# One scan stage's order rewritten: the inverse loaded and transposed just ahead of its products, and a later stage's first products taken two pieces at a time

## The chip, the cores and the metric

The kernel runs on one core of one Trainium2 chip. The metric is the time on the device in microseconds (us), as the median of several runs; lower is better.

## The reference, cut to what matters

One step of a diffusion backbone with one layer. From normalised and modulated tokens (128 context tokens, 2048 latent ones, 1024 channels) one input projection makes all operands. Half of the channels go through an RWKV-7 recurrence, in both directions, with 8 heads of 64 channels:

```python
def step(S, inp):
    r_t, w_t, k_t, v_t, kk_t, a_t = inp
    s_kk = jnp.einsum('bdhij,bdhj->bdhi', S, kk_t)
    S = (S * w_t[..., None, :] - s_kk[..., :, None] * (kk_t * a_t)[..., None, :]
         + v_t[..., :, None] * k_t[..., None, :])
    return S, jnp.einsum('bdhij,bdhj->bdhi', S, r_t)
s_final, ys = lax.scan(step, s0.astype(f32), xs)
```

The other half is a gated short convolution. Both are gated, joined, projected out, added to the input and normalised. Everything is in float32.

## The kernel before, in words

**Three phases.** `phase1` makes the projections and writes the operands of the recurrence to memory. `phase2` is the recurrence, called the scan here. `phase3` is the output projection; some of its products are made within the last stages of the scan.

**How the scan is cut.** The tokens are cut into chunks of 64, and the recurrence over a chunk becomes matrix products: within a chunk a triangular system is solved, and only the 64 x 128 state of a pair of heads is carried from chunk to chunk. There are 17 stages (`NST`, line 618); a stage is eight chunks of one pair of heads in each direction, so two groups `g` per stage, forward and backward. Of a stage `s` these parts exist, all generators that hand back control at each `yield`:

- `partL` (line 789) loads the operands `rr`. `partM` (807) makes masked products of them: F, GA and Q. One pass over a group is four pieces, given by `MORD`: both halves of F ("Ff"); both halves of GA and the packed blocks dg, which ScalarE's queue stores to memory ("GgD"); nothing; the transposes Q. Each piece starts from block-diagonal copies `bd` made by ScalarE. With two groups that is eight pieces. `partI` (845) loads the blocks back as `ab` (line 850, SyncE's queue), and GpSimd solves for the first half of the inverse, `zt`, in 15 rounds (lines 864 to 870), and stores it (line 871).
- `partW` (873) loads that part of the inverse as `zc` and transposes it on VectorE into `zr` (line 879); then, in two halves, it loads strips of operands (`load_stk`, lines 779 and 782) and copies parts of GA and Q into them, and loads the values `sv`.
- `partU` (899) uses `zr` in the small products psU (line 905), their copy and `zc` in the products psW (912), and writes the whole inverse `zb`.
- `partB` (924), in two halves of three pieces: psX from `zb` and F (931), copies into the strips by ScalarE, and the products psE (942), masked by VectorE into E (943).
- `partS` (947) is the recurrence itself, eight scan steps numbered from 0: psS from E and the state (982), and VectorE's scaling of the state for the next step (995). After steps 3 and 7 the outputs `y` are copied or added (`outputs`, line 1002); `finish` completes a block of outputs.

**What sets the order.** `main` (line 1085) writes the stages' parts into one another by hand. In stage `s` it takes the scan steps of `s`. Before step 0 and after each step, `emit(k)` takes what the string at place `k` of `ORDER` names: L a half of `partW` of stage s+1, b and B a piece of `partB` (of stage s, second half, and of s+1, first half), U a piece of `partU` of s+1. Ahead of that, after every scan step, one piece of `partM` of stage s+3 (`LA` is 3) is taken, and after it, where there is one, a part of `finish`. At the end of the stage come `partL` of s+4 and `partI` of s+3. Stage 15, the last that has a next one, goes by `ORDER_END`.

The order in the code is not quite the order in the engines' queues. The context is opened with `schedule_with_timeline_sim=True` (line 1334): a scheduler plays the program against its own estimate of durations and puts onto each engine's queue what is ready by that estimate, the earlier in the code first. Once it is in a queue, the order is fixed: an instruction that waits holds up all that stand behind it on its engine. SyncE's queue issues nearly all loads and stores.

**Rings that bind pieces to one another.** `zc` and `zr` have one buffer each; the PSUM pool of psF, psG and psQ has two banks, and so has the pool of psU, psW, psX, psE and of the transposes in `finish`. `bd` and `rr` have two tiles. F, GA and Q have three slots, so that a later stage's F waits until psX of the stage three before has read it.

Of the kernel before, what the change touches and what calls it, by code (L numbers as in the profile page):

```python
# [620 lines left out]
LA = 3  # L621


ORDER_END = ("LbbbL", "U", "U", "", "BBB", "", "", "", "")
ORDER = ("LbbbL", "", "U", "", "U", "", "BBB", "", "")


def phase2(K):
    nc, tc, A, S = K.nc, K.tc, K.A, K.S
    V, G, P, T = nc.vector, nc.gpsimd, nc.scalar, nc.tensor  # L630
    D = nc.sync.dma_start
    MF, MG, ME = (0, 1), (0, 1), (2, 3)
    B = Ctx()
    O = Ctx()
# [73 lines left out]
    def copy(k, dst, src, negate=False):  # L708
        if negate:
            if k in ON_DVE:  # L710
                V.tensor_scalar(dst, src, -1.0, None, ALU.mult)
            else:
                P.activation(dst, src, AF.Copy, scale=-1.0)
        else:
            (V.tensor_copy if k in ON_DVE else P.copy)(dst, src)  # L715
# [16 lines left out]
    def tl(shape, tag, b, pool=None, dt=F32):  # L732
        return (pool or O.l0).tile(shape, dt, tag=tag, name=f"{tag}_{K.u()}", bufs=b)
# [21 lines left out]
    def load_v(dst, units):  # L755
        if units[0][0] == units[-1][0]:
            p, c0 = units[0]
            D(dst.rearrange("t u h v -> t u (h v)"), S["vt"][c0 * 64:(c0 + 8) * 64, p * 128:(p + 1) * 128].rearrange("(u t) c -> t u c", t=64))
        else:
            for u in range(2):  # L760
                D(dst.rearrange("t (g u) h v -> t u g (h v)", u=2)[:, u], S["vt"][u * 64:u * 64 + 64, :].rearrange("t (g c) -> t g c", g=4))
# [7 lines left out]
    def load_stk(t_, g, k, us):  # L769

        units = g.units[us]
        p, c0 = units[0]
        src = S[f"ops{g.d}"][k]
        n = 4 if p == units[-1][0] else 2
        for i in range(4 // n):
            dst = t_[0:64, 1, :, us.start + n * i:us.start + n * (i + 1)]
            x = src[(p + i) * 128:(p + i + 1) * 128, c0 * 64:(c0 + n) * 64]
            if t_ is g.rt:
                D(dst.rearrange("c h u t -> c h (u t)"), x.rearrange("(h c) t -> c h t", h=2))
            else:  # L780
                for hd in range(2):
                    D(dst[:, hd], x[hd * 64:hd * 64 + 64].rearrange("c (u t) -> c u t", t=64))

    def half(g, n):

        h = n if g.d == 0 else 1 - n
        return slice(h * 4, h * 4 + 4)

    def partL(s):
        st = Ctx()  # L790
        st.g = []
        for gi, (d, units, blk) in enumerate(stages[s]):
            g = Ctx()
            st.g.append(g)
            g.d, g.units, g.blk = d, units, blk
            g.rr = B.rr()
            if blk is None:
                for i, k in ((0, 0), (1, 1), (3, 2), (4, 3)):
                    load(g.rr[:, i], d, k, units, FULL)
            else:  # L800
                p, c0 = units[0]
                src = S[f"ops{d}"][:, p * 128:(p + 1) * 128, c0 * 64:(c0 + 8) * 64]
                for i, k in ((0, 0), (3, 2)):
                    D(g.rr[:, i:i + 2].rearrange("p k u t -> p k (u t)"), src[k:k + 2].rearrange("k p t -> p k t"))
        return st
# [66 lines left out]

    def partW(s, st):

        st.zc = tl([128, 16, 32], "zc", 1, O.l1)
        for h in range(2):
            D(st.zc[h:128:2], S["zt"][s][h].rearrange("u s b q i -> (s b q) u i"))
        st.zr = tl([128, 16, 32], "zr", 1, O.l1)
        V.transpose(st.zr[:].rearrange("p u i -> p (u i)"), st.zc[:].rearrange("p u i -> p (u i)"))
        for g in st.g:  # L880
            g.lt, g.rt = B.lt(), B.rt()
            g.fs, g.gs = (g.lt, g.rt) if g.d == 0 else (g.rt, g.lt)
            g.E = []
        for n in range(2):
            for g in st.g:
                us = half(g, n)
                load_stk(g.fs, g, 2, us)
                load_stk(g.gs, g, 1, us)
                for i in range(2):
                    r = slice(64 - i * 64, 128 - i * 64)  # L890
                    copy("g", g.gs[64:128, 1, i, us], g.GA[r, us, 0:64])
                    k = us.start // 2
                    copy("h", g.gs[64:128, 0, :, us.start + i:us.stop:2], g.Q[i * 64:i * 64 + 64, k:k + 2].rearrange("p k (h c) -> p h k c", h=2))
                if n == 0:
                    g.sv = tl([128, 8, 2, 64], "sv", 4)
                    load_v(g.sv[64:128], g.units)
            yield

    def partU(s, st):

        pu = O.p2.tile([128, 16, 32], F32, tag="s", name=f"psU{s}")
        rows = [(slice(sl * 64, sl * 64 + 32), slice(sl * 64 + 32, sl * 64 + 64)) for sl in range(2)]
        for u in range(16):
            for r0, r1 in rows:
                T.matmul(pu[r1, u, :], st.g[u // 8].GA[r0, u % 8, 96:128], st.zr[r0, u, :], start=True, stop=True)
        for r0, r1 in rows:
            copy("u", B.bu[r1], pu[r1])
        yield
        pw = O.p2.tile([128, 16, 32], F32, tag="s", name=f"psW{s}")
        for u in range(16):  # L910
            for r0, r1 in rows:
                T.matmul(pw[r0, u, :], B.bu[r1, u, :], st.zc[r1, u, :], start=True, stop=True)
        zf = B.zb[:].rearrange("p d u c -> p (d u) c")
        for r0, r1 in rows:
            for r in (r0, r1):
                copy("z", zf[r, :, r], st.zc[r])
            copy("n", zf[r0, :, r1], pw[r0], True)
        yield
# [156 lines left out]
    def first(s):  # L1075
        sts[s] = partL(s)
        yield from partM(s, sts[s])
        partI(s, sts[s])
# [6 lines left out]
    def main():  # L1085
        setup_rest()
        run = lambda gen: [None for _ in gen]
        W = partW(0, sts[0])
        next(W)
        run(first(2))  # L1090
        sts[LA] = partL(LA)
        run(partU(0, sts[0]))
        bb = partB(0, sts[0])
        next(W)
        for _ in range(3):
            next(bb)
        tail = iter(())
        for s in range(NST):
            st = sts.pop(s)
            more = s + 1 < NST  # L1100
            W = partW(s + 1, sts[s + 1]) if more else iter(())
            uu = partU(s + 1, sts[s + 1]) if more else iter(())
            own, bb = bb, partB(s + 1, sts[s + 1]) if more else iter(())
            gens = dict(L=W, b=own, U=uu, B=bb)

            def emit(k):
                for c in (ORDER if s < NST - 2 else ORDER_END)[k]:
                    next(gens[c], None)

            if s < NST - 1:  # L1110
                emit(0)
            else:
                run(own)
            todo = [pend.pop(0) for _ in range(len(pend) if s > NST - 4 else min(1, len(pend)))]
            if s == NST - 3:
                O.pm.close()
                O.r2.close()
                O.r1.close()
                K.weights()
                tail = K.ahead()  # L1120
            if s == NST - 1:
                O.l1.close()
                run(tail)
                tail = K.tail()
            if s >= NST - 2:
                for f in todo:
                    run(f)
            m = partM(s + LA, sts[s + LA]) if s + LA < NST else iter(())
            for i, _ in enumerate(partS(s, st, sts.get(s + 1))):
                next(m, None)  # L1130
                next(tail, None)
                if s < NST - 1:
                    emit(i + 1)
                for f in todo[:1] if s < NST - 3 else todo:
                    next(f, None)
            for f in todo:
                run(f)
            run(m)
            if s + LA + 1 < NST:
                sts[s + LA + 1] = partL(s + LA + 1)  # L1140
            if s + LA < NST:
                partI(s + LA, sts[s + LA])
        for f in pend:
            for _ in f:
                pass
        for p in (O.pS, O.p2):
            p.close()
        K.rest(tail)
        for p in (O.l0, O.rI, O.r0):
            p.close()  # L1150

    K.early, K.main, K.spare = early, main, spare


# [184 lines left out]
```

## Time and profile before

| | us |
|---|---|
| median of 3 runs | 1802.34 |
| lowest and highest run | 1801.06, 1805.57 |
| the profiled execution's own time | 1795.1 |
| its span in the profile | 1793.3 |
| TensorE busy | 1654.0 |
| VectorE, ScalarE, GpSimd busy | 1151.0, 831.0, 594.5 |

The profile shows one execution. PE is TensorE's products, PEld its loads of weights, DVE VectorE, ACT ScalarE, POOL GpSimd and SPq the queue of SyncE. A row of the timeline has its start, its duration, the engine, the line of the kernel, the operation, output and inputs by name, and how many were joined into the row; in brackets is how long the engine stood idle before it, and what ended that. A row of waits has the total, how often, and the longest. The profile counts a product of float32 as two passes, so that a psS group of one direction is x4. The scan runs from about 1020 to 1635 us.

### The profile page before, as it was taken

Reading aid. Unit: us, or ns where it says so; the run is one execution under the profiler, and the core shown is the slowest. Engines: PE = TensorE matmul, PEld = TensorE weight load, DVE = VectorE, ACT = ScalarE, POOL = GpSimd, SP = SyncE. Lnnn points to the kernel's source line nnn. Section 1 sums busy time; section 2 is a strip of 40 time slices with the busy share of each in tenths; the row PEclk is TensorE's granted clock in tenths of the full one; section 3 lists DMA queues with packets and bytes.
Section 4 is the critical chain, followed back from the end, with each engine's and each line's share of the span. In section 5 each row is a group of like instructions: output and inputs, shape, how many; then the busy total and the mean of one; then the engine's idle time right before and its main releaser. Section 6 shows DMA issues by size and latency. Waiting matters only on the chain. (4 is left out here: it accounts for less than half of the span.)

```text
span 1793.3 us, 33024 instructions
## 1 busy us (share of the span) xinstructions
PE 1654.0 (92%) x12400; PEld 1562.5 (87%) x12400; DVE 1151.0 (64%) x2197; ACT 831.0 (46%) x1607; POOL 594.5 (33%) x1089
## 2 busy tenths in 40 slices
PE   5998899999899999999999898989999988989998
PEld 3988899899888999989899898889898988877886
DVE  5988896546677445477843466756766856666433
ACT  4565644215445122355421276656667665533222
POOL 0131210002222000122217257767667767223221
PEclk9999999999899999999999899999999998899999
DMA  9788786556788634478776476676567764546432
GB/s 358 217 243 233 238 271 236 198 211 167 172 186 192 190 119 145 136 211 249 212 240 241 112 175 153 159 180 171 154 173 183 182 171 101 158 139 210 151 135 102
DMA packets 315376, 335.16 MB, mean 187 GB/s; under 512 B 166920, under 2 KB 263560, under 8 KB 301136
## 3 DMA queue, kind: packets, MB, share of 16 engines
q1 hardware_dynamic: 242912, 323.99, 60.8%
q10 hardware_dynamic: 70944, 4.60, 2.9%
q0 software_dynamic: 1360, 4.46, 0.7%
q8 instruction: 98, 1.61, 0.4%
q14 instruction: 62, 0.51, 0.1%
HBM read 221.16 MB, written 111.82 MB: 186 GB/s over the span
## 5 line engine op out<-in xcount | busy, mean ns | idle before, releaser
L870 POOL TENSOR_TENSOR zt<-zt,ztmp 128x30 f32<-128x30 f32 (+7 forms) x510 | 196.9, 386 | 39.7
L942 PE MATMUL psE<-str,stl 128*128 128x128 f32 x1088 | 154.6, 290 | 24.8 <-DVE E L943 23.3
L942 PEld LDWEIGHTS psE<-str,stl 128*128 128x128 f32 x1088 | 140.0, 202 | 27.2 <-DVE E L943 24.5
L982 PE MATMUL psS<-sv,E 128*128 128x64 f32 x1088 | 152.3, 273 | 2.5 <-DVE sv L995 2.3
L982 PEld LDWEIGHTS psS<-sv,E 128*128 128x128 f32 x1088 | 144.0, 198 | 4.8 <-DVE sv L995 3.1
L867 POOL TENSOR_TENSOR ztmp<-ab,zt 128x60 f32<-128x60 f32 (+7 forms) x255 | 135.0, 529 | 19.7
L715 ACT COPY bd<-rr 64x512 f32<-64x512 f32 x136 | 83.9, 617 | 102.3 <-issue 45.2
L314 POOL TENSOR_TENSOR shk<-rawl 128x384 f32<-128x384 f32 (+1 forms) x24 | 19.7, 821 | 274.2 <-ACT rawl L310 268.4
L943 DVE TENSOR_TENSOR E<-psE,msk 128x512 f32<-128x512 f32 x136 | 93.2, 685 | 24.8 <-PE psE L942 22.7
L828 PE MATMUL psG<-rr,bd 128*128 128x128 f32 x544 | 79.6, 293 | 15.9 <-DVE GA L829 11.1
L995 DVE TENSOR_TENSOR sv<-psS,pc 64x128 f32<-64x128 f32 x254 | 67.8, 277 | 40.8 <-PE psS L982 39.0
L931 PE MATMUL psX<-F,zb 128*128 128x128 f32 x544 | 78.1, 296 | 9.4 <-DVE E L943 6.5
L1275 POOL TENSOR_TENSOR z<-z,x 128x512 f32<-128x512 f32 x32 | 43.6, 1366 | 128.3 <-DVE z L1271 106.5
L828 PEld LDWEIGHTS psG<-rr,bd 128*128 128x128 f32 x544 | 71.0, 204 | 17.1 <-DVE GA L829 11.9
L158 PE MATMUL mmv<-h,w 128*128 128x384 f32 (+1 forms) x192 | 69.0, 359 | 18.2 <-ACT q1r L312 9.6
L828 PE MATMUL psF<-rr,bd 128*128 128x128 f32 x544 | 79.3, 289 | 3.4 <-ACT bd L715 1.9
L931 PEld LDWEIGHTS psX<-F,zb 128*128 128x128 f32 x544 | 71.9, 209 | 11.0 <-DVE E L943 7.5
L828 PEld LDWEIGHTS psF<-rr,bd 128*128 128x128 f32 x544 | 70.3, 200 | 4.5 <-issue 2.1
L829 DVE TENSOR_TENSOR F<-psF,msk 128x512 f32<-128x512 f32 x68 | 46.5, 685 | 36.2 <-PE psF L828 22.0
L195 POOL TENSOR_TENSOR hsls<-sq,hshs 128x384 fp32r<-128x384 f32 (+1 forms) x24 | 31.5, 1312 | 110.6 <-DMA scr_vt<-vt 37.3
L158 PE MATMUL mmg<-h,w 128*128 128x384 f32 (+1 forms) x192 | 63.4, 330 | 4.9 <-ACT ta L374 2.9
L159 PE MATMUL mmv<-h,w 128*128 128x384 f32 (+1 forms) x192 | 66.9, 349 | 0.0
(308 smaller groups left out, 5199.8 us busy)
## 6 DMA issues: line engine op xcount, KB each, us to landing
w<-scr_wsp SPq DMA_DIRECT2D x68, 1024.0 KB, 6.7
scr_wsp<-w SPq DMA_DIRECT2D x34, 1024.0 KB, 6.3
rr<-scr_ops SPq DMA_DIRECT2D x64, 512.0 KB, 4.9
scr_ops<-sp SPq DMA_DIRECT2D x160, 192.0 KB, 4.7
wr<-in_win SPq DMA_DIRECT2D x34, 512.0 KB, 7.3
ab<-scr_at SPq DMA_DIRECT2D x34, 256.0 KB, 3.8
x<-in_x SPq DMA_DIRECT2D x17, 512.0 KB, 3.7
wadas<-in_wada SPq DMA_DIRECT2D x8, 1024.0 KB, 15.2
```

Of the source, the lines that this page charges most:

```text
L158: T.matmul(ps[:, :n], w[:, 0, k], hh[:, 0, k, :n], start=k == 0, stop=False)
L159: T.matmul(ps[:, :n], w[:, 0, k], hh[:, 1, k, :n], start=False, stop=False)
L715: (V.tensor_copy if k in ON_DVE else P.copy)(dst, src)
L828: T.matmul(ps[:, i, :].rearrange("p (a b) -> p a b", b=64), w[:, u, :], x[:, :, u, :], start=True, stop=True)
L829: V.tensor_tensor(dst[:, h * 4:h * 4 + 4, :], ps[:], mask.unsqueeze(1).broadcast_to((128, 4, 128)), ALU.mult)
L867: G.tensor_tensor(tv, ab[:, j:j + 2, j + 2:32].unsqueeze(1).broadcast_to((128, kn, 2, n)), zt[:, :kn, j:j + 2].unsqueeze(3).broadcast_to(( ...
L870: G.tensor_tensor(zt[:, :kn, j + 2:32], zt[:, :kn, j + 2:32], tv[:, :, r], ALU.subtract)
L931: T.matmul(px[:, i, :], B.zb[:, gi, us.start + i, :], g.F[:, us.start + i, :], start=True, stop=True)
L942: T.matmul(pe[:, i, hd, :].rearrange("p (b t) -> p b t", b=2), g.lt[:, :, hd, us.start + k + i].rearrange("p b t -> p (b t)"), g.rt[:, :, ...
L943: V.tensor_tensor(g.E[n][:, k:k + 2].rearrange("p a b c -> p (a b) c"), pe[:].rearrange("p a b c -> p (a b) c"), B.msk[:, ME[g.d]].unsquee ...
L982: T.matmul(sp[gi][:, q, hd, :], g.E[n][:, k, hd, :], sv[:, u, hd, :], start=True, stop=True)
L995: V.tensor_tensor(dst, sp[gi][0:64, q], B.pc[0:64, d, 2 * p:2 * p + 2, c:c + 1].broadcast_to((64, 2, 64)), ALU.mult)
```

## The change

No instruction is added or taken away. Four things are moved in the code's order:

1. The load of `zc` goes behind the first half of the strip loads and the loads of `sv` in `partW`.
2. The transpose `zr` leaves `partW` and becomes the first of now three pieces of `partU`.
3. In `ORDER`, the pieces of U stand after scan steps 1 (transpose), 2 (psU) and 4 (psW); before, psU stood after step 1 and psW after step 3, and the transpose before step 0. In `ORDER_END` transpose and psU stand after step 0 and psW after step 1, where psU stood after step 0 and psW after step 1.
4. The eight pieces of `partM` are taken two after each of the scan steps 0, 1 and 2 and one after each of the steps 3 and 4; before, one after each of the eight.

```diff
-ORDER_END = ("LbbbL", "U", "U", "", "BBB", "", "", "", "")
-ORDER = ("LbbbL", "", "U", "", "U", "", "BBB", "", "")
+ORDER_END = ('LbbbL', 'UU', 'U', '', 'BBB', '', '', '', '')
+ORDER = ('LbbbL', '', 'U', 'U', '', 'U', 'BBB', '', '')
...
     def partW(s, st):
 
-        st.zc = tl([128, 16, 32], "zc", 1, O.l1)
-        for h in range(2):
-            D(st.zc[h:128:2], S["zt"][s][h].rearrange("u s b q i -> (s b q) u i"))
-        st.zr = tl([128, 16, 32], "zr", 1, O.l1)
-        V.transpose(st.zr[:].rearrange("p u i -> p (u i)"), st.zc[:].rearrange("p u i -> p (u i)"))
...
                     load_v(g.sv[64:128], g.units)
+            if n == 0:
+                st.zc = tl([128, 16, 32], "zc", 1, O.l1)
+                for h in range(2):
+                    D(st.zc[h:128:2], S["zt"][s][h].rearrange("u s b q i -> (s b q) u i"))
             yield
 
     def partU(s, st):
 
+        st.zr = tl([128, 16, 32], "zr", 1, O.l1)
+        V.transpose(st.zr[:].rearrange("p u i -> p (u i)"), st.zc[:].rearrange("p u i -> p (u i)"))
+        yield
         pu = O.p2.tile([128, 16, 32], F32, tag="s", name=f"psU{s}")
...
             for i, _ in enumerate(partS(s, st, sts.get(s + 1))):
-                next(m, None)
+                for _ in range((2, 2, 2, 1, 1, 0, 0, 0)[i]):
+                    next(m, None)
```

## The prediction

> **What bounds the kernel now.** I read the page first, then the busy time by stretches, then who waits for whom, then the timeline of single stages of the scan.
>
> ```profile
> span 1793.3 us, 33024 instructions
> PE 1654.0 (92%) x12400; PEld 1562.5 (87%) x12400; DVE 1151.0 (64%) x2197; ACT 831.0 (46%) x1607; POOL 594.5 (33%) x1089
> ```
>
> TensorE is the busiest engine, so time is won only where TensorE stands still or runs slowly. The change touches only the scan. It has 17 stages; I count one from the products psU of one stage to those of the next. The views by stretches give 13 full stages together, and some of them singly (columns: length, busy time of PE, PEld, DVE, ACT, POOL, then the granted clock):
>
> ```profile
> 1059.42:1498.55 439.13, 399.05 (x4727) 389.64 (x4726) 301.00 (x649) 283.14 (x517) 318.29 (x707) 0.96 0.67 166
> ...
> 1157.93:1193.49 35.56, 32.18 (x370) 31.83 (x369) 25.17 (x52) 21.16 (x39) 26.44 (x59) 0.90 0.66 166
> 1193.49:1228.73 35.24, 31.49 (x374) 30.99 (x373) 22.32 (x50) 23.60 (x45) 24.14 (x54) 0.95 0.65 164
> 1365.34:1396.68 31.34, 29.54 (x360) 28.45 (x360) 21.86 (x49) 22.13 (x42) 22.98 (x52) 1.00 0.77 188
> 1396.68:1427.32 30.64, 29.09 (x359) 28.12 (x358) 25.06 (x56) 20.44 (x38) 22.27 (x51) 1.00 0.80 199
> 1427.32:1463.40 36.08, 31.94 (x369) 31.59 (x368) 25.11 (x52) 21.46 (x40) 27.18 (x61) 0.91 0.67 156
> ```
>
> The same work takes 30.6 us in one stage and 36.1 in the next. The mean is 439.13 / 13 = 33.8 us. Stages of 31 us have the full clock, those of 35 and more 0.90 to 0.95. The view of the waits, between 1020 and 1560 us (SyncE's from 890), says what the long stages have (total us, times, longest):
>
> ```profile
> DVE zr L879 <- DMA zc<-scr_zt: 36.1, 12, 5.2
> PE psE L942 <- DVE E L943: 23.3, 8, 4.1
> PE psG L828 <- DVE GA L829: 11.1, 4, 3.8
> PE psX L931 <- DVE E L943: 6.5, 6, 1.8
> SPq L877 <- DMA scr_zt<-zt: 24.7, 9, 7.0
> ```
>
> VectorE stands 36.1 us in front of the transpose zr, because the load of the inverse (zc) has not landed; that load itself stands on SyncE until GpSimd's store of the inverse has landed. TensorE's three large waits, 40.9 us together, are for mask products (E, GA) that VectorE makes. One stage shows that these are one event:
>
> ```profile
> 1198.63 0.61 POOL L871 DMA_DIRECT2D scr_zt<-zt  x1 [0.30 <-POOL zt L870]
> ...
> 1203.42 1.11 PE L828 MATMUL psG<-rr,bd 128*128 128x128 f32 x8
> 1203.59 1.48 SPq L877 DMA_DIRECT2D zc<-scr_zt  x2
> 1204.37 1.06 PE L942 MATMUL psE<-str,stl 128*128 128x128 f32 x8
> 1209.16 0.71 DVE L879 STREAM_TRANSPOSE zr<-zc 128x512 f32<-128x512 f32 x1 [5.11 <-DMA zc<-scr_zt]
> 1209.80 0.65 DVE L829 TENSOR_TENSOR GA<-psG,mkg 128x512 f32<-128x512 f32 x1
> 1210.51 2.07 PE L828 MATMUL psG<-rr,bd 128*128 128x128 f32 x8 [3.75 <-DVE GA L829]
> 1212.37 1.75 PE L942 MATMUL psE<-str,stl 128*128 128x128 f32 x8
> 1228.73 1.20 PE L905 MATMUL psU<-zr,GA 32*32 32x32 f32 x64
> ```
>
> VectorE idles 5.11 us. The GA mask, whose product was made at 1203.4, stands behind the transpose, both PSUM banks of psG are full, and TensorE waits 3.75 us. The products after that take 2.07 and 1.75 us against 1.11 and 1.06 before: 1.65 us more. And zr is read only at 1228.73, 19.6 us after it was begun: the wait buys nothing. The stage of 30.64 us is the counterproof:
>
> ```profile
> 1408.29 2.05 SPq L877 DMA_DIRECT2D zc<-scr_zt  x2
> 1414.16 0.70 DVE L879 STREAM_TRANSPOSE zr<-zc 128x512 f32<-128x512 f32 x1
> ```
>
> Here VectorE had other work ahead of zr, reached it 5.9 us after the load was issued, and did not wait; that stage took 30.64 us.
>
> **The change, part by part.** No instruction is added or removed; all is order.
>
> *The transpose, moved from the head of a stage to behind scan step 1.* In code order this puts VectorE work between its old place and the new one: four masks of E, four of F and GA, a dg, and four scan evictions. Their durations:
>
> ```profile
> L943 DVE TENSOR_TENSOR E<-psE,msk 128x512 f32<-128x512 f32 x136 | 93.2, 685 | 24.8 <-PE psE L942 22.7
> L829 DVE TENSOR_TENSOR F<-psF,msk 128x512 f32<-128x512 f32 x68 | 46.5, 685 | 36.2 <-PE psF L828 22.0
> L834 DVE SCALAR_TENSOR_TENSOR dg<-GA,hm,dg 128x256 f32<-128x256 f32 x34 | 20.8, 611 | 8.5 <-ACT dg L833 8.0
> L995 DVE TENSOR_TENSOR sv<-psS,pc 64x128 f32<-64x128 f32 x254 | 67.8, 277 | 40.8 <-PE psS L982 39.0
> ```
>
> That is 8 x 0.685 + 0.611 + 4 x 0.277 = 7.2 us, against a wait of 36.1 / 12 = 3.0 us and at most 5.2. If the queue keeps code order, every wait is covered and a stage costs about 31.0 us, the mean of the two shortest above: 13 x (33.8 - 31.0) = 36 us, the full gain. The rows forbid counting on all of it, because the engine queues do not keep code order:
>
> ```profile
> 1405.87 0.69 DVE L829 TENSOR_TENSOR F<-psF,msk 128x512 f32<-128x512 f32 x1 [0.94 <-PE psX L931]
> ...
> 1408.63 0.69 DVE L829 TENSOR_TENSOR GA<-psG,mkg 128x512 f32<-128x512 f32 x1
> ...
> 1410.78 0.69 DVE L1011 TENSOR_TENSOR y<-psS,y 64x512 f32<-64x512 f32 x1
> ```
>
> F and GA of the next stage's pieces run ahead of y, which closes the stage before. The scheduler puts what it holds ready into a gap. So zr may slide back by anything from 0 to 7.2 us. I take two thirds of the gain, 24 us: a slide of 2 us, or of one or two masks, already covers most waits of 3.0 us and takes the longest below the length at which TensorE slows down.
>
> *That slowing.* Rows of two other stages:
>
> ```profile
> 1142.94 1.16 PE L942 MATMUL psE<-str,stl 128*128 128x128 f32 x8 [1.89 <-DVE E L943]
> 1244.43 1.79 PE L828 MATMUL psG<-rr,bd 128*128 128x128 f32 x7 [2.23 <-DVE GA L829]
> ```
>
> After 1.89 us of waiting eight products take 1.16 us; after 2.23 us seven take 1.79. So a wait cut to under 2 us loses its price in clock even if it stays; the full gain above has this in it, since it is made from whole stages. The Trainium skill, in "TensorE: Matmul & The Clock Gate" ("What's actually happening"), puts the drop to half rate after an idle window of about 3.4 us. The trace agrees in kind (0.90 to 0.95 granted in the long stages) but shows it after 2.23 us already; the two rows psE and psG hold 12 waits of 34.4 us, 2.9 us in the mean, so by the page's figure about half of them would cost clock (an estimate: 6 x 1.65 = 10 us), by this trace nearly all of them (12 x 1.65 = 20 us). If only the clock's part were won, the gain would be the one or the other of these, 1792 or 1782 at the median.
>
> *The load zc, moved on SyncE behind six strip loads and the loads of v.*
>
> ```profile
> 1207.10 1.29 SPq L758 DMA_DIRECT2D sv<-scr_vt  x2
> ...
> 1216.51 1.26 SPq L782 DMA_DIRECT2D stl<-scr_ops  x2
> ...
> 1220.79 2.50 ACT L715 COPY zb<-zc 32x512 f32<-32x512 f32 x4
> ```
>
> Upper bound: SyncE keeps code order, zc is issued when the strips are through at 1217.8 and lands 5.6 us later (1203.59 to 1209.16 above), at 1223.4. psU at 1228.73 is still met; the four ScalarE copies of zc would slip by 2.6 us, with the bd copies and scan copies queued behind them: at most 2.6 x 15 = 39 us if all of it reached TensorE. Lower bound: the load goes out where it does today (it is ready when the strips are not), 0. The nearest row is today's, and ScalarE is busy only 283.14 of 439.13 us; I take 0. No gain is to be had here: zc waits for the store of the solve (24.7 us above), not for room on SyncE.
>
> *psU and psW one scan step later*: 31 / 8 = 3.9 us. I take 0, for the reason in the second rival.
>
> *The later stage's pieces two at a time.* Both groups' masks and dg come up to three scan steps (12 us) earlier in code order, so the block store, GpSimd's solve and the store of the inverse may also come earlier: from 0 to 12 us. It works on the 24.7 us that SyncE stands before zc, the same wait seen once more, so it adds no term; it is part of why I take two thirds and not one. Rings of buffers still hold the first pieces back: F at 1405.87 waited for psX.
>
> *Ends.* In the last stage that has a next one zr and psU stand side by side in the new order, so that psU could take over the wait: between 0 and 5.2 us. I take 0, because the later pieces are done by then and leave the queues emptier. Stages outside the 13 can give back a wait of 3.0 us: 0 to 3, I take 2. Sum: 24 + 2 = 26 us.
>
> **The rivals.** *The wait stays.* The scheduler gives zr the first gap after the moment at which it believes zc landed; it believed so 3 us too early before and still does. For it: F and GA running ahead. Against it: the 30.64 us stage, where three items more made the wait vanish. The load has gone back as far as the transpose, so VectorE waits the same: 0 to 9 us gained, 1793 to 1802 at the median, 1798 as its middle.
>
> *The other side: the first E of the next stage comes late.* psU, psW, psX and E follow one another and end in the next stage's first scan product:
>
> ```profile
> 1427.32 1.20 PE L905 MATMUL psU<-zr,GA 32*32 32x32 f32 x64
> ...
> 1430.53 0.69 DVE L1011 TENSOR_TENSOR y<-psS,y 64x512 f32<-64x512 f32 x1
> ...
> 1439.69 0.64 DVE L943 TENSOR_TENSOR E<-psE,msk 128x512 f32<-128x512 f32 x1
> ...
> 1445.93 0.65 DVE L1011 TENSOR_TENSOR y<-psS,y 64x512 f32<-64x512 f32 x1
> ```
>
> The stage's last y ends 6.3 us after the first E: that is the room. One scan step takes 3.9 us of it. The four F and GA groups that now stand ahead of psU take another 4 x 1.06 us on TensorE, or about twice that if each waits for its mask: 8 to 12 us in all. Beyond 6.3 us each us costs 15 us over the scan; it outweighs the 36 us gained from a delay of 6.3 + 36 / 15 = 8.7 us. At 10 us it gives 3.7 x 15 - 36 = +20: 1822. Against it: the queues run pieces ahead already, and the psU of this row runs beside scan step 3 (y at 1430.5 closes that step) though its code place is after step 1, counted from 0; the new code place, after step 2, is still no later than where it runs.
>
> **How the numbers follow.** The profiled execution took 1795.1 us, span 1793.3; the median of the runs is 1802.34, 7.2 us above. 1795.1 - 26 = 1769, at the median 1802.3 - 26 = **1776 us**. Forecast: chance 0.60, from 1759 (36 + 3, and every stage at 30.64: 13 x 0.36 = 5 more) to 1791 (a third of the gain). The wait stays: 0.22. Slower: 0.18, around 1822. The range 1759 to 1808 leaves out most of the last and little else. A measurement tells about 0.3% (5 us) from no change: faster 0.60 + 0.07 of the second case = 0.67; within 0.3% 0.15; slower 0.18.
>
> **What would show it.** Right: the wait of zr for zc falls from 36 to under 12 us; TensorE's waits for E and GA in the scan fall by over 25; stages of 31 to 32.5 us at a clock of 0.97 and more; the time before 1020 us unchanged. The rival of the wait: zr at the same distance behind zc, with 3 us idle. The other side: scan products psS waiting for E, psU after scan step 4. I am wrong if zr no longer waits and the stages still take 33.8 us: then TensorE had another limit just below.

## The result, and the profile after

| | median, us | lowest and highest run |
|---|---|---|
| before, 12 runs | 1801.53 | 1795.9, 1810.63 |
| after, 12 runs | 1804.97 | 1791.35, 1812.19 |

The ratio after to before is 1.0005, with a 95% interval of 0.9983 to 1.0027: no change that can be measured.

The page of after, from an execution of 1812.19 us:

```profile
span 1810.4 us, 33015 instructions
PE 1659.8 (92%) x12400; PEld 1568.3 (87%) x12400; DVE 1149.2 (63%) x2197; ACT 832.6 (46%) x1607; POOL 593.8 (33%) x1089
```

The execution profiled is one of the slowest of its twelve, and its span is 17.1 us over that of before. Nearly all of this lies ahead of stage 1 of the scan: its psU starts at 1075.32 us, at 1059.42 in before and between 1056.9 and 1063.3 in every kernel below. So only the scan is compared. Busy time by stretches, first the same 13 stages together, then three of them:

```profile
1075.32:1516.69 441.37, 399.95 (x4726) 390.09 (x4725) 300.58 (x649) 284.46 (x517) 317.93 (x706) 0.95 0.66 165
...
1247.44:1278.85 31.41, 29.21 (x366) 28.57 (x365) 21.82 (x50) 23.13 (x43) 22.16 (x49) 1.00 0.75 185
1278.85:1313.86 35.01, 30.09 (x359) 29.35 (x358) 24.55 (x56) 20.65 (x38) 25.38 (x55) 0.90 0.62 167
1313.86:1351.09 37.23, 32.67 (x381) 32.05 (x381) 25.94 (x55) 22.33 (x43) 27.28 (x62) 0.95 0.68 170
```

441.37 us against 439.13: 34.0 us a stage against 33.8. Short stages with the full clock and long ones with less still follow one another. TensorE's idle time, length less PE's busy time, is 41.4 us against 40.1. The waits between 1020 and 1560 us (SyncE's from 890) show why:

```profile
PE psE L944 <- DVE E L945: 18.1, 8, 4.6
...
PE psX L933 <- ACT zb L713: 9.6, 7, 3.4
PE psX L933 <- DVE E L945: 8.4, 7, 5.5
PE psQ L821 <- DVE GA L829: 5.4, 2, 4.9
...
DVE zr L901 <- DMA zc<-scr_zt: 40.2, 13, 5.1
...
SPq L895 <- DMA scr_zt<-zt: 26.0, 8, 7.7
```

The wait that the change was priced on is still there: 40.2 us where it was 36.1, once more often. So is what follows from it on TensorE, now spread over psE, psX and psQ. One stage of the timeline, put beside that of before:

```profile
1322.19 0.62 POOL L871 DMA_DIRECT2D scr_zt<-zt  x1 [0.30 <-POOL zt L870]
...
1326.16 1.60 SPq L895 DMA_DIRECT2D zc<-scr_zt  x2
...
1326.68 0.69 DVE L945 TENSOR_TENSOR E<-psE,msk 128x512 f32<-128x512 f32 x1 [0.20 <-PE psE L944]
...
1332.52 0.71 DVE L901 STREAM_TRANSPOSE zr<-zc 128x512 f32<-128x512 f32 x1 [5.14 <-DMA zc<-scr_zt]
...
1333.98 0.69 DVE L945 TENSOR_TENSOR E<-psE,msk 128x512 f32<-128x512 f32 x1
...
1334.73 2.08 PE L944 MATMUL psE<-str,stl 128*128 128x128 f32 x8 [4.56 <-DVE E L945]
...
1351.09 1.20 PE L907 MATMUL psU<-zr,GA 32*32 32x32 f32 x64
```

It is the picture of before. After one mask E, VectorE goes to the transpose, stands 5.14 us until zc lands, and the next mask comes 7.3 us after the one before it; TensorE waits 4.56 us, and its next eight products take 2.08 us. zr is read 18.6 us after it was begun. In code order the transpose now stands behind scan step 1; on VectorE it does not.

**Where the transpose stands in the queue.** An engine's queue is fixed when the kernel is built, so it can be listed. Counted in VectorE operations, zr of a stage (stages 2 to 15) stands this far behind the first of the eight masks E of the running stage, the one before it (four belong to its first half, four to its second); a negative number is ahead of it:

```
            stage 2   3   4   5   6   7   8   9  10  11  12  13  14  15   mean
before         14  10   9   4  -3  -2   3   3  -1  -2   7   3  -3   2    3.1
after          16   9   8   2  -1   2   5   1  -1   2  12   3  -3  -1    3.9
```

The whole move in the code came out as 0.7 of an operation a stage. VectorE's operations in the scan take 301.00 / 649 = 0.46 us each, so zr slid back by 0.3 us, where up to 7.2 had been reckoned with. Nor had zr stood where the code had it: there it came just ahead of the second half's four masks E, but in the queue of before it stood 17.2 operations ahead of the first of these, in the mean. In after, where the code has it behind all four, it stands 16.0 ahead.

### The profile page after: what moved, and what is told of

The parts are those of the page before. It is cut to its first block, busy times and chain, and to the rows that moved or that the text cites. A ratio compares the mean times of both kernels' runs of the same rounds, so it can differ in the third digit from the quotient of the medians.

```text
span 1810.4 us, 33015 instructions
## 1 busy us (share of the span) xinstructions
PE 1659.8 (92%) x12400; PEld 1568.3 (87%) x12400; DVE 1149.2 (63%) x2197; ACT 832.6 (46%) x1607; POOL 593.8 (33%) x1089
## 5 line engine op out<-in xcount | busy, mean ns | idle before, releaser
L870 POOL TENSOR_TENSOR zt<-zt,ztmp 128x30 f32<-128x30 f32 (+7 forms) x510 | 201.1, 394 | 39.8
L715 ACT COPY bd<-rr 64x512 f32<-64x512 f32 x136 | 84.2, 619 | 89.7 <-issue 31.6
L314 POOL TENSOR_TENSOR shk<-rawl 128x384 f32<-128x384 f32 (+1 forms) x24 | 19.6, 818 | 279.2 <-ACT rawl L310 279.1
L933 PE MATMUL psX<-F,zb 128*128 128x128 f32 x544 | 86.7, 318 | 19.3 <-ACT zb L713 10.9
L933 PEld LDWEIGHTS psX<-F,zb 128*128 128x128 f32 x544 | 78.5, 226 | 22.1 <-ACT zb L713 11.6
L158 PE MATMUL mmv<-h,w 128*128 128x384 f32 (+1 forms) x192 | 70.7, 368 | 23.9 <-ACT q1r L312 13.9
L828 PE MATMUL psG<-rr,bd 128*128 128x128 f32 x544 | 75.3, 285 | 4.8 <-DVE F L829 4.8
L160 PE MATMUL mmv<-h,w 128*128 128x384 f32 (+1 forms) x192 | 68.8, 358 | 0.1
L159 PE MATMUL mmv<-h,w 128*128 128x384 f32 (+1 forms) x192 | 68.8, 358 | 0.0
L829 DVE TENSOR_TENSOR F<-psF,msk 128x512 f32<-128x512 f32 x68 | 46.5, 685 | 34.9 <-PE psF L828 22.4
```

The source lines that it names most:

```text
L158: T.matmul(ps[:, :n], w[:, 0, k], hh[:, 0, k, :n], start=k == 0, stop=False)
L159: T.matmul(ps[:, :n], w[:, 0, k], hh[:, 1, k, :n], start=False, stop=False)
L160: T.matmul(ps[:, :n], w[:, 1, k], hh[:, 0, k, :n], start=False, stop=k == 7)
L828: T.matmul(ps[:, i, :].rearrange("p (a b) -> p a b", b=64), w[:, u, :], x[:, :, u, :], start=True, stop=True)
L870: G.tensor_tensor(zt[:, :kn, j + 2:32], zt[:, :kn, j + 2:32], tv[:, :, r], ALU.subtract)
L933: T.matmul(px[:, i, :], B.zb[:, gi, us.start + i, :], g.F[:, us.start + i, :], start=True, stop=True)
```

## The experiments

The theory after the result: the gain is there, but only where zr stands later in VectorE's queue, and code order doesn't put it there, because the scheduler places zr into the first gap after the moment at which it believes zc landed. Against it stood: TensorE has another limit just below, so that a later zr wins nothing; the load itself comes later in the new order and eats the gain; the change's two halves, each with an effect of its own, cancel. All kernels of a group ran beside before, whose median was 1792.84, 1792.51 and 1793.37 us in the three groups (1 to 4, 5 to 8, 9 to 12). Gains in us below are the ratio's distance from 1 times that median.

| | ratio to before [95%] | median, us | 13 stages, us | PE busy | PE idle | wait of zr for zc from 1020 to 1560 us, us (times) | zr's place, mean |
|---|---|---|---|---|---|---|---|
| before | | | 439.13 | 399.05 | 40.1 | 36.1 (12) | 3.1 |
| after | 1.0005 [0.9983, 1.0027] | 1804.97 | 441.37 | 399.95 | 41.4 | 40.2 (13) | 3.9 |
| 1 after, zr behind last mask | 0.9878 [0.9854, 0.9903] | 1768.81 | 417.08 | 390.33 | 26.8 | 2.2 (1) | 31.8 |
| 2 before, the same | 0.9935 [0.9914, 0.9956] | 1782.23 | 430.68 | 406.15 | 24.5 | none | 31.6 |
| 3 pieces alone | 0.9968 [0.9945, 0.9991] | 1784.66 | 435.98 | 397.62 | 38.4 | 39.4 (13) | 2.1 |
| 4 inverse alone | 1.0056 [1.0035, 1.0077] | 1800.67 | 448.20 | 405.92 | 42.3 | 33.7 (12) | 6.1 |
| 5 after, zr behind second mask | 0.9892 [0.9872, 0.9912] | 1770.04 | 422.23 | 399.82 | 22.4 | 2.3 (1) | 21.4 |
| 6 as 2, with pieces | 0.9907 [0.9871, 0.9943] | 1775.13 | 421.72 | 394.61 | 27.1 | none | 32.2 |
| 7 before, inverse of stage 0 | 0.9945 [0.9921, 0.9968] | 1781.37 | 429.98 | 396.07 | 33.9 | 42.3 (15) | -4.6 |
| 8 as 5, first state ordered | 0.9851 [0.9831, 0.9872] | 1765.19 | 412.06 | 396.25 | 15.8 | 2.4 (1) | 21.4 |
| 9 load moved alone | 0.9999 [0.9974, 1.0023] | 1791.19 | 445.28 | 407.06 | 38.2 | 36.7 (12) | 4.1 |
| 10 places of U alone | 0.9988 [0.9967, 1.0008] | 1789.68 | 435.58 | 400.81 | 34.8 | 25.8 (11) | 5.0 |
| 11 as 8, load early | 0.9831 [0.9799, 0.9863] | 1761.65 | 410.93 | 394.18 | 16.8 | none | 21.4 |
| 12 no transpose | 0.9906 [0.9873, 0.9939] | 1774.16 | 417.83 | 393.37 | 24.5 | | |

Ratio and median are over the runs of a kernel; the columns behind them are from its one profile.

**1. After, with zr tied behind the last mask of the stage.**

```diff
         st.zr = tl([128, 16, 32], "zr", 1, O.l1)
-        V.transpose(...)
+        with (K.tc.issue_after(prev.lastE.ins) if prev else ExitStack()):
+            V.transpose(...)
...
-                    V.tensor_tensor(g.E[n][:, k:k + 2]..., ALU.mult)
+                    st.lastE = V.tensor_tensor(g.E[n][:, k:k + 2]..., ALU.mult)
```

`issue_after` adds no wait; it tells the scheduler that on the same queue zr stands behind that instruction, the last mask E of the running stage's second half.

> The changed kernel, with one thing more: on VectorE's queue the transpose zr is ordered behind the last mask E of the second half, where the code order seemed to put it (order in the queue only, no new data). Theory A, the scheduler fills zr into the first gap after the moment at which it believes zc landed, so the code order hardly moved it and the wait stayed: the wait of VectorE for zc falls from 40.2 us to under 3, TensorE's waits for E, GA and zb in the scan fall by 25 or more, stages of 31 to 32 us instead of 34.0, and the time falls by 25 to 40 us (ratio 0.978 to 0.987). Theory B, TensorE has another limit just below, or psU now waits for zr: the wait for zc goes as well, but the stages still take 33 us or more and the ratio stays within 0.995 to 1.01.

Measured: 0.9878, 22 us. Of the waits for zc one is left, of 2.2 us. The 13 stages, then two waits of TensorE, then the one long stage that is left (1253.55 to 1292.30, 38.75 us):

```profile
1062.12:1479.20 417.08, 390.33 (x4720) 380.21 (x4721) 305.49 (x649) 284.10 (x516) 314.58 (x695) 0.98 0.70 175
```

```profile
PE psX L934 <- DVE E L946: 11.9, 14, 5.0
PE psU L908 <- DVE zr L902: 11.6, 15, 1.8
```

```profile
1269.02 0.66 SPq L977 DMA_DIRECT2D sv<-in_st  x1
...
1273.21 0.28 DVE L979 TENSOR_REDUCE mn<-sv 64x2 f32<-64x128 f32 x1 [5.04 <-DMA sv<-in_st]
...
1275.28 2.08 PE L934 MATMUL psX<-F,zb 128*128 128x128 f32 x8 [4.97 <-DVE E L946]
...
1291.53 0.71 DVE L902 STREAM_TRANSPOSE zr<-zc 128x512 f32<-128x512 f32 x1
```

So theory A holds in the main: the same code with zr further back in the queue has a gain, a little under the 25 to 40 us expected, and TensorE's waits for E, GA and zb fall from 41.5 us (the four rows of after) to 19.6, by 21.9 where 25 was expected. The scheduler did reorder other work along with zr: of VectorE's other 635 operations in the 13 stages, 557 stand in the same order as in after. Two things are left in it. The transpose is now a little too late (psU waits 11.6 us), and where a new pair of heads begins, the mean `mn` of its first state waits on VectorE for its own fresh load (5.04 us), with the same masks behind it: the same fault with another operation.

**2. Before, with zr tied in the same way.** The transpose goes from `partW` into the first piece of `partU`, behind the last mask; load, places of U and pieces stay those of before.

```diff
     def partW(s, st):
...
-        st.zr = tl([128, 16, 32], "zr", 1, O.l1)
-        V.transpose(...)
...
     def partU(s, st, prev=None):
 
+        st.zr = tl([128, 16, 32], "zr", 1, O.l1)
+        with (K.tc.issue_after(prev.lastE.ins) if prev else ExitStack()):
+            V.transpose(...)
```

> The kernel before, in which only the transpose is taken into the first piece of partU and ordered on VectorE's queue behind the last mask E of the second half; the load of zc, ORDER and the pieces of partM stay as they were. Theory A: as good as the same edit in the changed kernel, 25 to 40 us faster (ratio 0.978 to 0.987), since the place in the queue is all that counts. Rival: the pieces two at a time and the later load are needed to have the inverse in time; then VectorE's wait for zc stays at 10 us or more, or psU waits, and less than half of the gain shows (ratio above 0.99).

Measured: 0.9935, 12 us, under half of the 25 to 40 that theory A expected, so the place of zr is not all that counts; the ratio is the rival's, and psU does wait for zr (12.9 us, none in before), but it does so in 1 too. The wait for zc is gone here, and TensorE's idle time is as low as in 1 (24.5 us against 26.8); but TensorE is busy 15.8 us longer with the same work, at a clock of 0.95 against 0.98. One stage takes 38.21 us with 0.7 us of idle time:

```profile
1123.23:1161.44 38.21, 37.52 (x376) 36.35 (x376) 25.82 (x58) 22.48 (x40) 30.51 (x71) 0.82 0.57 153
```

```profile
1123.23 1.34 PE L906 MATMUL psU<-zr,GA 32*32 32x32 f32 x64 [1.66 <-DVE zr L901]
...
1125.40 3.73 PE L828 MATMUL psF<-rr,bd 128*128 128x128 f32 x16
...
1159.29 2.22 PE L828 MATMUL psF<-rr,bd 128*128 128x128 f32 x16
```

Sixteen products of psF take 3.73 us behind a psU that waited 1.66 us, and 2.22 us at the stage's end. In the record of the granted clock, 2 spends 44.4 us of its 13 stages at half clock and 1 spends 17.1; half of that difference, 13.7 us, is most of the 15.8. Four of the eight falls in 2 come right after a psU that waited 1.1 to 1.9 us for zr, in 1 one of four. Why so many more here, with psU's waits alike (12.9 us in 2, 11.6 in 1), is not settled.

**3 and 4. Each half of the change alone.** 3 has the pieces of `partM` two at a time and nothing else; 4 has all the rest.

```diff
             for i, _ in enumerate(partS(s, st, sts.get(s + 1))):
-                next(m, None)
+                for _ in range((2, 2, 2, 1, 1, 0, 0, 0)[i]):
+                    next(m, None)
```

> The kernel before with only the pieces of partM two at a time. Theory A: the queues run these pieces ahead as the rings allow, whatever the code says, so no more than 0.3% either way (0.997 to 1.003), the wait for zc 30 to 42 us. Rival C, the two halves of the change cancel: this half loses 5 us or more (1.003 and above) by putting masks ahead of the scan, or gains 5 us or more.

> The changed kernel with the pieces of partM one at a time again, so the move of the load, of the transpose and of the pieces of U alone. Theory A: within 0.3% of before (0.997 to 1.003), with a wait for zc of 30 to 42 us, because the transpose goes one mask further back at most. Rival C, the halves cancel: 5 us or more faster (0.997 and below) with a wait under 25 us, the loss then lying in the pieces two at a time.

Measured: 0.9968 and 1.0056, so some 6 us faster and 10 us slower (1792.84 x 0.0032 and x 0.0056). Neither is within theory A's 0.3%, though 3 only just. The wait of zr is in both. The rows of 3 and of 4:

```profile
DVE zr L879 <- DMA zc<-scr_zt: 39.4, 13, 7.3
```

```profile
DVE zr L901 <- DMA zc<-scr_zt: 33.7, 12, 5.9
...
PE psX L933 <- DVE E L945: 29.2, 17, 6.0
```

The two halves partly cancel, but with the signs the other way round than the expectation of 4 had it: 0.9968 x 1.0056 = 1.0024, within the interval of the whole change. But neither takes the wait away, so this is beside the cause. In 4, 6.9 of the 9.1 us by which its 13 stages are longer are busy time of TensorE.

**5. Only two masks back.** As 1, but behind the second of the second half's four masks, so that zr isn't late for psU.

```diff
-        with (K.tc.issue_after(prev.lastE.ins) if prev else ExitStack()):
+        with (K.tc.issue_after(prev.mask[1, 0].ins) if prev else ExitStack()):
```

> The changed kernel with zr ordered on VectorE's queue behind the second of the four masks E of the second half, instead of behind the last one. Behind the last, psU waited 11.6 us for zr in all. Theory A, psU's wait was the price of standing too late and nothing else: zr still waits under 4 us for zc, psU's wait falls under 3 us, and the time falls by 5 to 10 us against the kernel with the last mask (ratio to before 0.982 to 0.986). Rival: the wait only goes back to zc or on to psX, and the ratio stays at 0.988 or above.

Measured: 0.9892, no faster than 1. The wait of psU for zr fell from 11.6 us to 1.6, and the idle time from 26.8 to 22.4 us, but the time did not follow, since TensorE was busy 9.5 us longer, with 37.6 us at half clock against 17.1. The rival's ratio holds, but not its reason: zr waits 2.3 us for zc, and psX's wait for E fell from 11.9 us to 6.4. What psU waited was not what kept 1 from the full gain.

**6. Before, with the last mask and with pieces two at a time.** This is 2 and 3 together.

> The kernel before with the pieces of partM two at a time and zr ordered behind the last mask E; the load of zc and the strings of U stay as before. Against the changed kernel with the same order of zr (0.9878) it lacks the move of the load and of U; against the kernel before with that order alone (0.9935) it has the pieces added. If the pieces and the place of zr are all that counts: 0.985 to 0.990, and ScalarE's wait for zc, 10.9 us with the later load, falls under 3 us. If the move of the load or of U helps: 0.991 or more.

Measured: 0.9907, its interval reaching into those of both 1 and 2: it doesn't say which part of the change makes 1 better than 2. ScalarE's wait for zc did fall, to 1.4 us. The first state's wait is large here:

```profile
DVE mn L978 <- DMA sv<-in_st: 18.5, 4, 6.4
```

**7. Before, but every stage loads the inverse of stage 0.** This load never has to wait for a store of this stage.

```diff
-            D(st.zc[h:128:2], S["zt"][s][h].rearrange(...))
+            D(st.zc[h:128:2], S["zt"][0][h].rearrange(...))
```

> The kernel before, but every stage loads the inverse of stage 0, so zc never waits for GpSimd's store of its own stage (the scan's values are those of the wrong inverse; all operations stay). Theory A1, the wait of zr is the delay that the whole chain store, load, solve, store, load has picked up against the scheduler's plan: the wait of VectorE for zc falls from 36 us to under 10 and the time by 15 us or more (ratio under 0.992). Theory A2, the single load of zc takes longer than the scheduler believes: the wait stays at 20 us or more and the ratio within 0.995 to 1.005.

```profile
DVE zr L879 <- DMA zc<-scr_zt: 42.3, 15, 5.5
PE psS L982 <- DVE sv L995: 12.9, 6, 3.5
...
PE psG L828 <- DVE GA L829: 6.9, 3, 3.7
PE psE L942 <- DVE E L943: 6.7, 6, 3.1
PE psX L931 <- DVE E L943: 6.6, 11, 1.3
```

The load is issued earlier now (in the mean 26.9 us ahead of its psU, 21.1 in before), and the scheduler moves zr forward with it (4.6 operations ahead of the first mask, where it was 3.1 behind); the wait stays, 42.3 us in 15 waits, 2.8 us each. So the chain of solve, store and load isn't needed for the wait. In 7 as in before the load lands later than zr's place allows for, and zr follows the load. The time falls by 10 us (0.0055 x 1792.5) although VectorE's wait does not: theory A2 is right on the wait and just misses on the time. The rows show where they are won. TensorE's waits for E and GA come to 20.2 us, against 40.9 in before, while those of psS grew from 2.3 to 12.9. So the price is not VectorE's idle time itself but what TensorE needs of the work that stands behind it.

**8. As 5, with the first state's three operations tied as well,** behind the last mask of the first half of their own stage.

```diff
                         mn = tl([64, 2], "mn", 2)
-                        V.tensor_reduce(mn[:], x, mybir.AxisListType.X, ALU.add)
-                        ...
+                        with K.tc.issue_after(st.mask[0, 1].ins):
+                            V.tensor_reduce(mn[:], x, mybir.AxisListType.X, ALU.add)
+                            ...
```

> As the kernel with zr behind the second mask, and the three small VectorE operations on a first state, which stood up to 5 us for the load of that state in the kernel with the last mask, ordered behind the last mask E of their own stage's first half. Theory A, any VectorE operation on a fresh load placed by the scheduler stands the same way: those waits go and the time falls by another 4 to 10 us (ratio to before 0.977 to 0.983). Rival, there are too few of them (three stages) or the recurrence now waits for its state: within 4 us of the kernel with the second mask.

```profile
1059.86:1471.92 412.06, 396.25 (x4741) 385.09 (x4741) 307.52 (x653) 284.56 (x519) 319.14 (x699) 0.98 0.70 177
```

Measured: 0.9851, some 7 us better than 5 (0.41% of 1792.5), with intervals that just touch. `mn` no longer waits for its load. The 4 to 10 us that theory A wanted are there; the ratio is short of its range, which had been set for a better 5. TensorE's idle time is 15.8 us, the lowest of all.

**9 and 10. The parts of 4.** 9 moves load and transpose together behind the strips and leaves U where it was; 10 makes the transpose the first piece of U at U's new places and leaves the load at the head.

> The kernel before with only the load of zc, and the transpose right behind it, moved behind the first half of the strip loads and the loads of sv in partW. The inverse's half of the change alone lost 0.56%. If the later load is the loss: ratio 1.003 to 1.009, with larger waits of ScalarE or VectorE for zc. If the places of U are the loss: within 0.997 to 1.003.

> The kernel before with the transpose as the first piece of partU and the new strings ORDER and ORDER_END; the load of zc stays at the head of partW and the pieces of partM stay one at a time. If the places of U are the loss of the inverse's half: ratio 1.003 to 1.009, with psX waiting for the masks E by over 20 us as in that half (29.2). If the load is: within 0.997 to 1.003. In both cases zr waits for zc by 30 us or more, since the scheduler places it as before.

Measured: 0.9999 and 0.9988, both no change; zr waits 36.7 and 25.8 us, the second under the 30 expected. So neither move costs by itself, and the 10 us that 4 loses come only with both together; through what is open.

**11. As 8, with the load of zc back at the head of `partW`.**

> The kernel with zr behind the second mask and the first state's operations ordered too (0.9851), with the load of zc back at the head of partW. There ScalarE's copies of zc waited some 10 us for it. If the later load costs something: 0.978 to 0.983 and ScalarE's wait under 4 us; if SyncE sends it out at the same moment anyway: within 0.983 to 0.987.

```profile
1058.91:1469.84 410.93, 394.18 (x4742) 382.36 (x4741) 308.51 (x653) 284.58 (x519) 319.40 (x699) 0.99 0.71 177
```

```profile
PE psX L934 <- ACT zb L713: 7.3, 9, 1.3
PE psX L934 <- DVE E L946: 6.7, 13, 1.1
PE psG L829 <- DVE F L830: 4.8, 1, 4.8
```

Measured: 0.9831, 30 us: the best ratio of all. The longest wait of TensorE but for one of 4.8 us is near 2 us, and the clock is 0.99. ScalarE's wait for zc is 1.7 us, 8.3 in 8. Whether the early load adds to 8 isn't told: the intervals overlap. In the 13 stages the two kernels have one and the same order on VectorE, ScalarE and (but for one group) TensorE; only SyncE's differs, by 4 of 334 loads and stores.

**12. Before without the transposes; psU reads zc.**

```diff
-        st.zr = tl([128, 16, 32], "zr", 1, O.l1)
-        V.transpose(...)
...
-                T.matmul(pu[r1, u, :], ..., st.zr[r0, u, :], start=True, stop=True)
+                T.matmul(pu[r1, u, :], ..., st.zc[r0, u, :], start=True, stop=True)
```

> The kernel before without the transpose: psU reads zc itself (so the values of the inverse's other half are wrong, and 17 transposes of 0.71 us are left out; no order is imposed). It prices the wait with its consequences. Theory A, the wait of zr is what makes the stages long: 20 to 40 us faster (ratio 0.978 to 0.989), and TensorE's waits for E and GA fall by 25 us or more. Rival, once zr is gone the next operation on a fresh load takes its place: less than 10 us, ratio above 0.9945.

```profile
DVE mn L974 <- DMA sv<-in_st: 15.1, 5, 7.4
```

```profile
1268.29 2.08 PE L929 MATMUL psX<-F,zb 128*128 128x128 f32 x8 [7.11 <-DVE E L941]
```

Measured: 0.9906, 17 us, between theory A and the rival. Taking the operation away wins no more than putting it in the right place did in 1, since the next operation on a fresh load takes over: `mn` waits 15.1 us, once 7.4, and TensorE behind it 7.11.

## Why the prediction was wrong

**The reading of the bound was right.** VectorE's wait for zc makes TensorE wait and costs clock. No run moves zr and nothing else, since the scheduler reorders other work each time. What carries the reading is that the kernels part into two groups. Where zr is tied or left out (1, 2, 5, 6, 8, 11, 12), it waits 2.4 us at most, TensorE's idle time is 15.8 to 27.1 us, and the time falls by 0.65 to 1.7%. In the others (before, after, 3, 4, 7, 9, 10) zr waits 25.8 to 42.3 us, the idle time is 33.9 to 42.3, and no gain is over 0.55%. In idle time the groups lie apart; in time 2 and 7 overlap: 2 loses by its clock and in 7 less of what TensorE needs stands behind zr. Reordering alone doesn't do it: 3 has 567 of VectorE's 635 other operations in the order of before, about as 1 has against after, and gains 0.32%.

**The step that failed is the transpose's slide:** "zr may slide back by anything from 0 to 7.2 us. I take two thirds of the gain, 24 us". It slid by 0.3 us and gained nothing. The lower end was the right one, for the reason that the text itself gave against counting on all of it: the scheduler fills gaps. The two thirds had no row behind them; they assumed that zr started from its old place in the code, which it did not, and that code order counts for something between operations that wait for different things. The queue shows that here it counted for next to nothing; that the scheduler held zr ready at nearly the same moment as before is the likely reason, and in 7, where the load can go earlier, zr does go forward with it. So "the wait stays", given 0.22, is what happened, with its mechanism and with its sign in the profile, zr at the same distance behind zc with 3 us idle (40.2 / 13 = 3.1).

**What spoke against that rival was misread.** The stage of 30.64 us was taken as a sign that three operations more are enough, so that a move in the code would often do it. But three operations more in one stage say nothing of what a move in the code will do. After has such stages too: 3 of its 17 transposes start without a wait for zc, in before 5 of 17, and the other stages pay as before.

**The size of the full gain was too large for zr alone.** 36 us were reckoned; tying zr gave 22 (1) and 19 (5) in the new order and 12 in the old (2). 30 were won in 11 and 27 in 8, where a stage takes 31.6 and 31.7 us in the profile, against the 31.0 of the prediction, but a part of that belongs to the first state's `mn`, which the prediction hadn't seen.

**The slowing** was right in kind: TensorE's clock is 0.98 to 0.99 in 1, 8 and 11, against 0.95 to 0.96 in before and after; it is 0.95 to 0.97 in 2, 5 and 6, which gain less. Its price per wait was not: "under 2 us" is no safe limit (1.66 us ahead of psU in 2 were followed by 13.65 us at half clock), and 3.4 us no sure loss for the products right behind it. Before itself had spoken against the first: a psX there waited 1.83 us, and half clock followed from 1080.70 to 1084.12. (The row of seven products in 1.79 us is part of one of eight in 2.00.) From after:

```profile
1401.62 1.16 PE L944 MATMUL psE<-str,stl 128*128 128x128 f32 x8 [3.85 <-DVE E L945]
...
1404.01 1.92 PE L933 MATMUL psX<-F,zb 128*128 128x128 f32 x8
```

After 3.85 us of waiting the first eight products still run at 1.16 us; the slow ones come 2.4 us later. The Trainium skill, in "TensorE: Matmul & The Clock Gate" ("What's actually happening"), has the clock set by what a window of about 3.4 us held. The traces agree: in the scan of all of them the granted clock changes only in steps of 3.41 us. Two such steps of after, then two of 2 (columns as above, the clock third from the end):

```profile
1399.43:1402.84 3.41, 1.22 (x11) 1.22 (x11) 2.50 (x5) 0.62 (x2) 2.86 (x8) 1.00 1.04 217
1402.84:1406.25 3.41, 3.41 (x18) 3.41 (x18) 3.22 (x9) 1.98 (x5) 2.94 (x7) 0.50 1.17 252
```

```profile
1120.70:1124.11 3.41, 1.75 (x65) 1.64 (x64) 3.29 (x7) 1.82 (x3) 2.94 (x7) 1.00 0.69 159
1124.11:1127.52 3.41, 3.41 (x34) 3.35 (x28) 1.62 (x4) 1.66 (x3) 2.94 (x7) 0.50 0.69 266
```

A step with little work is followed by one at half clock, so what a wait costs depends on where it falls in the steps. The wait of 3.85 us is cut at 1399.43, and the clock falls only at 1402.84, behind the first eight products. In 2, half of the step's 1.75 us of products are psU's. Over all 14 traces, from 1030 to 1480 us, 50 of the 52 steps at full clock in which products other than psU and psW fill less than 0.4 are followed by half clock, 43 of the 344 between 0.4 and 0.7, and none of the 1251 above. With psU and psW counted in, 21 of the 1516 steps above 0.7 are, so these small products count for little.

**The zeros.** The load moved on SyncE: right by itself (9, 0.9999). psU and psW later: right by itself (10, 0.9988). Both together lose 10 us (4), which the prediction hadn't, and the cause is open. Pieces two at a time had no term of their own; they are worth some 6 us (3), at the edge of what was measured. The ends: psU waits for zr once in after, 1.2 us at the start of the scan, and not at the end, so the 0 was right. The rival on the other side did not come: TensorE waits no more for E than before (psE and psX together 26.5 us between 1020 and 1560 us, 29.8 before).

## What to carry to other kernels

Where a scheduler fixes the engines' queues, a move in the code need not be a move on the engine: list the queue before pricing it, and if an operation on a fresh load stands ahead of urgent ones, tie it behind the one that it must not hold up (here 22 us with this change's order, 12 without it). Then look for the next operation on a fresh load; here it was the first state's mean, and tying that too brought 27 us.

## What the runs showed of the hardware

- The load of zc takes 2.6 to 5.6 us from issue to landing in before, 3.7 in the median, and 3.3 to 6.2 in 7, where no store holds it up: VectorE stood 42.3 us in 15 waits there, 2.8 us each, about as much as before.
- The same TensorE work in 13 stages had a busy time of between 390.3 and 407.1 us, 4%. It follows the idle time only loosely: 2 and 12 have the same 24.5 us idle and 406.2 and 393.4 us busy. It follows the time at half clock, 44.4 us in 2 and 13.7 in 12. One profile's stage length says less than the ratio over many runs.
- The clock can fall with hardly any idle time: in 2 a stage with 0.7 us idle was granted 0.82. It fell at 1124.11, during psU, 64 products of 32 x 32, behind a wait of 1.66 us, and stayed at half for four steps of 3.41 us in which TensorE was busy throughout.
